# Entry of the feed-forward block: out-projection blocks in pair order, operand factors on VectorE alone, the first four up-projection blocks by direct products

## The chip, the cores and the metric

The kernel runs on one core of one Trainium2 chip. The metric is the device time of one execution in microseconds. TensorE (PE) multiplies into PSUM; VectorE (DVE), ScalarE (ACT) and GpSimd (POOL) do the elementwise work; transfers are issued by SyncE (SP).

## The reference, cut to what matters

One inference step of a two-layer decoder: 512 prompt tokens and 8 sample tokens, model width 1024, feed-forward width 4096, everything in float32. Layer 0 mixes by retention and memory attention, layer 1 by windowed attention and memory attention. Each layer then ends in the same way:

```
x = x + concat(mixer outputs) @ w_out        # the out-projection, 1024 x 1024
h = rmsnorm(x, g_mlp) @ w_up                  # 1024 -> 4096
x = x + square(relu(h)) @ w_down              # 4096 -> 1024
```

## The kernel before

Activations lie transposed: `x[kt]` is block kt (0 to 7) of 128 features by 520 tokens. All products are made of float32 values that are cut into a high part in a shorter format (a cast on ACT) and a low part (the remainder, a subtraction on DVE or POOL). Three products, high by high, high by low and low by high, replace one. Weights come by DMA as a raw block of 128 x 1024, and `chunk` cuts them in the same way (cast on line 215, remainder on line 216). There are three buffers for raw weights and three for each part.

**Out-projection.** `project` computes one output block of 128 features: 8 input blocks by 3 products for tokens 0 to 255, and the same for tokens 256 to 519, so 48 products a block. `residual` (line 434, DVE) adds each half to `x[mb]`. Layer 0 takes the blocks in the order 0 to 7. In layer 1 the first halves of blocks 0 to 6 are placed among the attention (`project_out(mb, 0)`), the second halves of these seven follow, and block 7 comes last with both halves.

**Feed-forward.** 32 up blocks are worked in four groups of eight, `up(g)`, and each group goes through `down(g)` while the next goes up. Only `up(0)` has no `down` beside it. Two up blocks are computed by `seven`: the 2 x 2 block form of a matrix product with seven sub-products in place of eight. Each sub-product is `times` (line 296): 4 input blocks by 3 products of 260 tokens, so 84 products for a pair. Sums of weight blocks are made by `total` (line 318, mostly POOL), and `parts` cuts them (cast 312, remainder 313).

The seven forms of the activations are made once per layer by `operands`. For each feature block, `y = x[kt] * gain * scale` (line 276, DVE, 520 wide), where `scale` is a factor left by the layer's first norm. From blocks j and j+4 it makes seven forms of 260 tokens: three are parts of y, four are sums or differences (`combine`, line 264). Each is cut by `cut` (cast 253 on ACT, remainder 254 on DVE or POOL by the string `ENG_L`). Of a block 0 to 3 two forms can be made alone; five forms need the second of the pair, block 4 to 7.

**Norm.** `rms` squares each `x[kt]` on ACT (line 376) and sums the squares (line 380), on the engine named by `ENG_R['f']`: POOL for blocks 1 to 6, DVE for block 7. `finish` reduces the sum over partitions on PE (line 390), runs thirteen small DVE steps (lines 393 to 361), transposes on PE (line 405) and writes the scale `r` on ACT (line 407). It is called after the first pair has been multiplied; then `u = max(u, 0) * r` (line 801, DVE), a square on ACT (line 802) and `hid.put` (cast 178, remainder 179) give the input of `down`.

**Order.** The program is handed to a planner that fixes each engine's queue before the run, by its own estimate of when things will be ready; each engine then takes its queue in order. Four PSUM banks of the kinds "mm" (three) and "ws" (two, one of which is meant here) take the up products.

Of the kernel before, what the change touches and what calls it, by code (L numbers as in the profile page):

```python
# [13 lines left out]
F32R = mybir.dt.float32r  # L14
I32 = mybir.dt.int32
AF = mybir.ActivationFunctionType
ALU = mybir.AluOpType
AX = mybir.AxisListType

P = 128  # L20
D = 1024
KT = D // P
# [8 lines left out]
SH = 12  # L31
FFG = 4
FK = 8
UK = KT // 2
EPS = 1e-6
NEG = -1e30
DK = P ** -0.5
# [2 lines left out]
ROLE_7 = ('mm', 'mm', 'ws')  # L40
BUFS_F = dict(blk=2, u=5, t=5, ws=2)
ROLE_D = ('wt', 'ot')
ORDER_F = "uddudduddudd"
ENG_UL = "vvvvvvvv"
ENG_T = "vvvp"
ENG_L = "vvpppvp"
ENG_R = dict(a='ppppvppv', m='pppppppv', f='pppppppv', b='vvvvvpvv', y='vppppppv')
ENG_B = "pvvvvvvv"
ENG_W = "pvppppvp"
BUFS_W = dict(wr=3, wh=3, wl=3)  # L50
# [66 lines left out]
def build(tc, d, o):  # L117
    nc = tc.nc
    with ExitStack() as ctx:
# [20 lines left out]
        def half(name, dt=F32, shape=None):  # L140
            return hp.tile(shape or [P, 4, TT], dt, name=name, tag="half")
# [58 lines left out]
        def gain(name, kt):  # L200
            return gains[:, GAINS.index(name), kt:kt + 1]
# [18 lines left out]
        def weights(*args, **kw):  # L220
            w, fill = chunk(*args, **kw)
            fill()
            return w

        def part(name, s, role="mm"):
            return ps(f"{name}{s}", role)[:, :HALVES[s].stop - HALVES[s].start]

        def product(t, w, act, b, s, order, nb, k):

            wh, wl = w  # L230
            for kt in order:
# [18 lines left out]
        def cut(op, j, src, eng):  # L250

            h, l = op[:, 0, j, :], op[:, 1, j, :]
            nc.scalar.copy(out=h, in_=src)  # L253
            eng.tensor_sub(out=l, in0=src, in1=f(h))  # L254

        def operands(name, g, scale):


            op, first = {}, {}
            left, right = slice(0, EVEN), slice(EVEN, TT)  # L260

            def combine(i, j, x0, x1, alu):
                t = blk(f"{name}t{i}{j}", [P, EVEN], "t")
                engine(ENG_T, (5, 7, 6, 4).index(i)).tensor_tensor(out=t, in0=x0, in1=x1, op=alu)  # L264
                put(i, j, t)
                return t

            def put(i, j, src):
                if i not in op:
                    op[i] = half(f"{name}{i}", F32R, [P, 2, UK, EVEN])  # L270
                cut(op[i], j, src, engine(ENG_L, i - 1))

            for kt in range(KT):
                j = kt % UK
                y = blk(f"{name}xg{kt}", tag="u")
                nc.vector.scalar_tensor_tensor(out=y, in0=x[kt], scalar=gain(g, kt), in1=scale, op0=ALU.mult, op1=ALU.mult)
                if kt < UK:
                    first[j] = y
                    put(1, j, y[:, left])
                    combine(5, j, y[:, right], y[:, left], ALU.subtract)  # L280
                else:
                    b11, b12, b21, b22 = first[j][:, left], first[j][:, right], y[:, left], y[:, right]
                    t = combine(7, j, b22, b12, ALU.subtract)
                    t = combine(6, j, t, b11, ALU.add)
                    put(3, j, b22)
                    combine(4, j, b21, t, ALU.subtract)
                    put(2, j, b21)
            return op
# [121 lines left out]
        def rms(name, tag="blk"):  # L410
            m = Rms(TT, TT // 5, name, tag)
            for kt in range(KT):
                m.add(kt, x[kt])
            return m
# [371 lines left out]

        def mlp(l, last):
            before, scale = now["norm"]
            op = operands(f"f{l}", f"mlp{l}", scale)
            m = rms(f"f{l}")  # L790
            r = []

            def up(g, hid):

                for n in range(0, FK, 2):
                    u = [blk(f"u{l}{g}{n}{i}", tag="u") for i in range(2)]
                    seven([d["w_up"][l, g * FK + n + i] for i in range(2)], op, u, f"u{l}{g}{n}", n // 2)
                    if not r:
                        r.append(m.finish(before)[1])
                    for i in range(2):  # L800
                        nc.vector.scalar_tensor_tensor(out=u[i], in0=u[i], scalar=0.0, in1=r[0], op0=ALU.max, op1=ALU.mult)  # L801
                        nc.scalar.square(out=u[i], in_=u[i])  # L802
                        hid.put(n + i, u[i])
                    yield

            def down(g, hid):

                for mb in range(KT):
                    w = weights(d["w_down"][l, g, mb], FK * P, f"d{l}{g}{mb}")
                    for s, ts in enumerate(HALVES):  # L810
                        t = part(f"d{l}{g}{mb}", s, ROLE_D[s])
                        product(t, w, hid, 0, s, range(FK), 1, range(FK))
                        residual(mb, ts, t)
                    yield

            def down_last(g, hid):

                ws = []
                for mb in range(KT):
                    t = half(f"dw{mb}", F32R, [P, 2, FK * P])  # L820
                    ws.append(weights(d["w_down"][l, g, mb], FK * P, f"d{l}{g}{mb}", [t[:, 0], t[:, 1]]))
                norm = iter(())
                for s, ts in enumerate(HALVES):
                    n = ts.stop - ts.start
                    m = Rms(n, n // 4, f"y{s}", "t", s == 1)
                    for mb in range(KT):
                        t = part(f"d{l}{g}{mb}", s)
                        product(t, ws[mb], hid, 0, s, range(FK), 1, range(FK))
                        residual(mb, ts, t)
                        m.add(mb, x[mb][:, ts])  # L830
                        nc.scalar.mul(out=x[mb][:, ts], in_=x[mb][:, ts], mul=gain("final", mb))
                        next(norm, None)
                    norm = final(m, s, ts)
                for _ in norm:
                    pass


            high = now["w"].tile([P, 4, 4, TT], F32R, name=f"hid{l}")

            def room(g):  # L840
                hid = Pair(f"hid{l}{g}")
                if g % 2:
                    hid.t.update({(part, i): high[:, 2 * j + i] for j, part in enumerate("hl") for i in range(2)})
                return hid

            hids = [room(g) for g in range(FFG)]
            for _ in up(0, hids[0]):
                pass
            for g in range(1, FFG):
                run(ORDER_F, u=up(g, hids[g]), d=down(g - 1, hids[g - 1]))  # L850
            if last:
                down_last(FFG - 1, hids[FFG - 1])
            else:
                for _ in down(FFG - 1, hids[FFG - 1]):
                    pass
# [9 lines left out]
        def layer_a():  # L865
# [55 lines left out]
            def memory():  # L921
# [4 lines left out]

            run(ORDER_A, h=heads(), g=(gate(h) for h in range(RH)), m=memory(), k=(step for l in range(2) for step in mem_kv(l)),
                s=mem_sample(0, qm, out), a=mem_attention(0, qm, out))
            for mb in range(KT):
                for _, ts, t in project(d["w_out_a"][mb], out, f"oa{mb}", [6, 7, 0, 1, 2, 3, 4, 5]):  # L930
                    residual(mb, ts, t)

        def layer_b():
# [44 lines left out]
            order = [6, 7, 0, 1, 2, 3, 4, 5]  # L978
            ahead = []

            def project_out(mb, s):

                if s == 0:
                    t = half(f"obw{mb}", F32R, [P, 2, KT * P]) if mb < KEEP else None
                    ahead.append(weights(*src(mb), t if t is None else [t[:, 0], t[:, 1]], nc.gpsimd if mb in POOL_W else nc.vector))
                t = part(f"ob{mb}", s)
                product(t, ahead[mb], out, 0, s, order, 1, order)
                residual(mb, HALVES[s], t)

            run(ORDER_B, k=(project_kv(i) for i in range(4)), q=(project_q(i) for i in range(6)),  # L990
                w=win_pair(0, q, kT[0], vt, out, ROLE_W), W=win_pair(1, q, kT[1], vt, out, ROLE_W),
                s=mem_sample(1, qm, out), S=win_sample(q, kT, vs, out), a=mem_attention(1, qm, out),
                o=(project_out(mb, 0) for mb in range(KEEP + 3)))
            for mb in range(KEEP + 3):
                project_out(mb, 1)
            for mb in range(KEEP + 3, KT):
                for _, ts, t in project(d["w_out_b"][mb], out, f"ob{mb}", order):
                    residual(mb, ts, t)

# [93 lines left out]
```

## Time and profile before

| | |
|---|---|
| median of three runs | 1249.92 us (1249.6 to 1253.53) |
| profiled execution, its time | 1251.94 us |
| profiled execution, its span | 1250.2 us |
| mean granted TensorE clock | 0.977 of full speed |

The profile is of one execution. Its time is 1.7 us above its span, which is what lies around the instructions. Times in rows are counted from the start of the span.

### The profile page before, as it was taken

The numbers are of one execution on the slowest core, as the hardware profiler recorded it, in microseconds if no ns is written. First come the engines' busy times: TensorE is split into PE (matmuls) and PEld (weight loads), VectorE is DVE, ScalarE is ACT, GpSimd is POOL, SyncE is SP. The second block draws the span as 40 slices with busy tenths as digits, with TensorE's granted clock in tenths as the row PEclk, the third lists the DMA queues.
The fourth block names the chain that finished last, engine by engine and source line by source line (L and its number), as shares of the span: only waits on it lengthen the run. The fifth ranks groups of instructions, "written<-read, shape, count | busy, mean of one in ns | idle before, by whom it ended". The sixth has DMA issues, their size and how long they took to land. (4 is left out here: it accounts for less than half of the span.)

```text
span 1250.2 us, 23651 instructions
## 1 busy us (share of the span) xinstructions
PE 1200.6 (96%) x9670; PEld 1140.9 (91%) x9670; DVE 853.5 (68%) x1563; ACT 537.6 (43%) x1007; POOL 310.0 (25%) x271
## 2 busy tenths in 40 slices
PE   8999999997999999999999998898999999999996
PEld 7999989997999999999999785577899999999996
DVE  7676767779876656676467548559996676666733
ACT  6232432334554444444324325554464444444532
POOL 3201100048321212121024113117632121121112
PEclk9999999999999999999999999889699999999998
DMA  8345522220222223232324353100122232322412
GB/s 306 106 154 175 201 77 85 73 85 34 102 102 102 101 86 102 85 119 85 119 85 137 103 185 128 42 1 35 51 102 102 85 118 85 105 99 92 143 37 69
DMA packets 43788, 128.25 MB, mean 103 GB/s; under 512 B 5112, under 2 KB 10368, under 8 KB 43552
## 3 DMA queue, kind: packets, MB, share of 16 engines
q1 hardware_dynamic: 41440, 119.80, 28.0%
q0 software_dynamic: 2240, 6.95, 1.5%
q8 instruction: 76, 1.25, 0.4%
q14 instruction: 32, 0.26, 0.1%
HBM read 117.65 MB, written 9.08 MB: 101 GB/s over the span
## 5 line engine op out<-in xcount | busy, mean ns | idle before, releaser
L434 DVE TENSOR_TENSOR xs<-d,xs 128x264 f32<-128x264 f32 (+1 forms) x128 | 53.9, 422 | 103.2 <-PE d L234 103.2
L802 ACT ACTIVATE u<-u 128x520 f32<-128x520 f32 x64 | 40.7, 636 | 30.3 <-DVE u L801 30.3
L234 PE MATMUL d<-hid,dw 128*128 128x256 f32 (+1 forms) x384 | 46.9, 283 | 0.0
L234 PEld LDWEIGHTS d<-hid,dw 128*128 128x128 f32 x384 | 46.3, 188 | 0.1
L635 POOL DMA_DIRECT2D out_ret_s<-s x12 | 6.8, 569 | 135.5 <-DVE s L634 102.8
L801 DVE SCALAR_TENSOR_TENSOR u<-u,f1r 128x520 f32<-128x520 f32 x32 | 30.0, 941 | 1.2 <-ACT f1r L407 0.8
L801 DVE SCALAR_TENSOR_TENSOR u<-u,f0r 128x520 f32<-128x520 f32 x32 | 29.7, 932 | 0.4
L701 POOL TENSOR_SCALAR wp<-wp,wsm 128x256 f32<-128x256 f32 (+1 forms) x32 | 15.5, 496 | 55.7 <-ACT wp L696 25.7
L234 PE MATMUL ob<-obh,obw 128*128 128x256 f32 (+1 forms) x128 | 26.7, 295 | 2.1 <-ACT obh L178 1.2
L696 ACT ACTIVATE wp<-wp,wnm 128x256 f32<-128x256 f32 (+1 forms) x48 | 22.5, 470 | 11.3 <-DVE wes L693 7.4
L234 PEld LDWEIGHTS ob<-obh,obw 128*128 128x128 f32 x128 | 21.0, 192 | 4.7 <-ACT obh L178 2.7
L179 DVE TENSOR_TENSOR hid<-u,hid 128x520 fp32r<-128x520 f32 x32 | 23.3, 729 | 0.0
L520 ACT ACTIVATE p<-ms,nm 128x256 f32<-128x256 f32 x32 | 14.8, 475 | 18.5 <-DVE nm L518 16.8
L709 PEld LDWEIGHTS wt<-c,wp 128*128 128x128 f32 x84 | 9.9, 148 | 12.6 <-POOL wp L701 6.6
L709 PE MATMUL wt<-c,wp 128*128 128x128 f32 x84 | 16.1, 302 | 5.1 <-POOL wp L701 3.5
L178 ACT CAST hid<-u 128x520 fp32r<-128x520 f32 x32 | 20.1, 628 | 0.9
L234 PE MATMUL ob<-obl,obw 128*128 128x256 f32 (+1 forms) x64 | 18.2, 299 | 0.8 <-DVE obl L179 0.7
L254 POOL TENSOR_TENSOR f<-f0t,f 128x260 fp32r<-128x260 f32 x12 | 11.8, 982 | 27.8 <-ACT f L253 27.8
L518 DVE TENSOR_REDUCE nm<-ms 128x2 f32<-128x512 f32 x16 | 10.3, 685 | 11.8 <-PE ms L499 11.8
L253 ACT CAST f<-f0t 128x260 fp32r<-128x260 f32 x16 | 6.5, 407 | 26.7 <-DVE f0t L264 26.7
L179 DVE TENSOR_TENSOR obl<-wo,obh 128x128 fp32r<-128x128 f32 x24 | 6.9, 287 | 15.1 <-ACT obh L178 15.0
L499 PE MATMUL ws<-kvb,qb 64*128 64x256 f32 (+1 forms) x96 | 15.6, 407 | 1.1 <-DVE wp L686 0.6
(2056 smaller groups left out, 5220.7 us busy)
## 6 DMA issues: line engine op xcount, KB each, us to landing
kc<-in_mem_k SPq DMA_DIRECT2D x16, 256.0 KB, 4.9
vc<-in_mem_v SPq DMA_DIRECT2D x16, 256.0 KB, 5.2
s<-in_S SPq DMA_DIRECT2D x12, 256.0 KB, 5.5
out_ret_s<-s POOLq DMA_DIRECT2D x12, 256.0 KB, 2.6
xs<-in_xT SPq DMA_DIRECT2D x8, 260.0 KB, 4.3
memx<-in_memT SPq DMA_DIRECT2D x1, 1024.0 KB, 8.8
u000r<-in_w_up SPq DMA_DIRECT2D x2, 512.0 KB, 3.2
u002r<-in_w_up SPq DMA_DIRECT2D x2, 512.0 KB, 3.2
```

Of the source, the lines that this page charges most:

```text
L178: nc.scalar.copy(out=self.hi(kt, sl, rows), in_=src)
L179: eng.tensor_sub(out=self.lo(kt, sl, rows), in0=src, in1=f(self.hi(kt, sl, rows)))
L234: nc.tensor.matmul(t, w[:, ws], a(kt, HALVES[s]), start=kt == k[0] and m == 0, stop=kt == k[-1] and m == 2)
L254: eng.tensor_sub(out=l, in0=src, in1=f(h))
L434: nc.vector.tensor_add(out=x[mb][:, ts], in0=t, in1=x[mb][:, ts])
L499: i = m()
L520: nc.scalar.activation(out=t[:, b, :], in_=s[hh][:, b, :], func=AF.Exp, bias=nm[:, b:b + 1], accum_out=sm[:, b:b + 1])
L696: nc.scalar.activation(out=pv[:, j, :], in_=pv[:, j, :], func=AF.Exp, bias=nm[:, j:j + 1], accum_out=sm[:, j:j + 1])
L701: (nc.gpsimd if j % 3 in POOL_N else nc.vector).tensor_scalar(out=pv[:, j, :], in0=pv[:, j, :], scalar1=sm[:, j:j + 1], scalar2=1.0, op0=A ...
L709: nc.tensor.transpose(t[:, i * P:i * P + P], p[:, 3 * hh + i, kk * P:kk * P + P], ident)
L801: nc.vector.scalar_tensor_tensor(out=u[i], in0=u[i], scalar=0.0, in1=r[0], op0=ALU.max, op1=ALU.mult)
L802: nc.scalar.square(out=u[i], in_=u[i])
```

## The change

The out-projection of both layers takes its blocks in the order 0, 4, 1, 5, 2, 6, 3, 7 (`BY_PAIR`), and `operands` makes its forms in that order. All remainders and combinations of `operands` and all sums of squares of this norm go to DVE; POOL has none of them. For each block `operands` also cuts the whole `y` (520 wide) into a `Pair` named `xg`, and hands `x[kt]` to the norm in the same loop. In `up(0)` the first four blocks are computed by `product` from `xg`, as an out-projection block is: 48 products each, into four PSUM banks by turns; they are evicted with the norm's `r` by one DVE operation per half. `seven` computes the last two pairs of `up(0)` and all pairs of the other groups. The buffer `high`, which held groups 1 and 3 of the hidden values, is made earlier and also holds `xg`.

```diff
+DIRECT = 2
+BY_PAIR = [kt + i * UK for kt in range(UK) for i in range(2)]
+ROLE_U = ('mm', 'mm', 'mm', 'ws')
-ENG_T = "vvvp"
-ENG_L = "vvpppvp"
-ENG_R = dict(a='ppppvppv', m='pppppppv', f='pppppppv', b='vvvvvpvv', y='vppppppv')
+ENG_R = dict(a='ppppvppv', m='pppppppv', f='vvvvvvvv', b='vvvvvpvv', y='vppppppv')
...
-        def operands(name, g, scale):
+        def operands(name, g, scale, direct, norm):
...
-                engine(ENG_T, (5, 7, 6, 4).index(i)).tensor_tensor(out=t, in0=x0, in1=x1, op=alu)
+                nc.vector.tensor_tensor(out=t, in0=x0, in1=x1, op=alu)
...
-                cut(op[i], j, src, engine(ENG_L, i - 1))
+                cut(op[i], j, src, nc.vector)
-            for kt in range(KT):
+            for n, kt in enumerate(BY_PAIR):
                 j = kt % UK
                 y = blk(f"{name}xg{kt}", tag="u")
                 nc.vector.scalar_tensor_tensor(out=y, in0=x[kt], scalar=gain(g, kt), in1=scale, op0=ALU.mult, op1=ALU.mult)
+                direct.put(kt, y)
+                norm.add(n, x[kt])
...
+            xg = room(f"xg{l}", True)
+            m = Rms(TT, TT // 5, f"f{l}", "blk")
+            op = operands(f"f{l}", f"mlp{l}", scale, xg, m)
...
-                for n in range(0, FK, 2):
+                n0 = 2 * DIRECT if g == 0 else 0
+                for n in range(n0):
+                    w = weights(d["w_up"][l, g * FK + n], D, f"u{l}{g}{n}")
+                    t = [part(f"u{l}{g}{n}", s, ROLE_U[(2 * n + s) % len(ROLE_U)]) for s in range(2)]
+                    for s in range(2):
+                        product(t[s], w, xg, 0, s, BY_PAIR, 1, BY_PAIR)
+                    if not r:
+                        r.append(m.finish(before)[1])
+                    u = blk(f"u{l}{g}{n}", tag="u")
+                    for s, ts in enumerate(HALVES):
+                        nc.vector.scalar_tensor_tensor(out=u[:, ts], in0=t[s], scalar=0.0, in1=r[0][:, ts], op0=ALU.max, op1=ALU.mult)
+                    nc.scalar.square(out=u, in_=u)
+                    hid.put(n, u)
+                    yield
+                for n in range(n0, FK, 2):
...
-            for mb in range(KT):
+            for mb in BY_PAIR:
                 for _, ts, t in project(d["w_out_a"][mb], out, f"oa{mb}", [6, 7, 0, 1, 2, 3, 4, 5]):
                     residual(mb, ts, t)
...
-            def project_out(mb, s):
+            def project_out(n, s):
+                mb = BY_PAIR[n]
...
-            for mb in range(KEEP + 3, KT):
+            for mb in BY_PAIR[KEEP + 3:]:
```

## Rows read from the trace of the kernel before

**Rows 1.** the profile page, busy time of each engine (us, share, instructions)

```profile
PE 1200.6 (96%) x9670; PEld 1140.9 (91%) x9670; DVE 853.5 (68%) x1563; ACT 537.6 (43%) x1007; POOL 310.0 (25%) x271
```

**Rows 2.** busy time by stretch; start:end, length, busy (instructions) of each engine, granted clock

```profile
294.70:328.50 33.80, 27.14 (x182) 25.57 (x181) 29.50 (x44) 16.10 (x33) 20.97 (x16) 0.85 0.14 47
328.50:351.80 23.30, 20.94 (x170) 20.32 (x169) 23.27 (x26) 14.64 (x25) 9.65 (x6) 1.00 0.27 92
351.80:361.90 10.10, 10.10 (x86) 10.10 (x86) 8.43 (x14) 6.94 (x13) 0.00 (x0) 1.00 0.33 115
868.20:906.50 38.30, 30.45 (x181) 28.81 (x181) 35.42 (x50) 18.16 (x39) 26.87 (x22) 0.73 0.14 46
906.50:929.80 23.30, 20.92 (x170) 20.29 (x169) 23.27 (x26) 14.63 (x25) 9.73 (x6) 1.00 0.26 91
```

**Rows 3.** PE's longest wait at the second entry (total us, times, longest)

```profile
PE u100b L296 <- DVE xs L434: 5.1, 1, 5.1
```

**Rows 4.** timeline, last out-projection product of layer 1, start and us

```profile
867.99 0.28 PE L234 MATMUL ob<-obh,ob7l 128*128 128x264 f32 x1
```

**Rows 5.** timeline of DVE at the second entry, residual sums

```profile
849.01 0.77 DVE L434 TENSOR_TENSOR xs<-ob,xs 128x264 f32<-128x264 f32 x2 [0.60 <-PE ob L234]
...
874.93 0.41 DVE L434 TENSOR_TENSOR xs<-ob,xs 128x256 f32<-128x256 f32 x1
```

**Rows 6.** timeline of DVE in layer 0's out-projection

```profile
272.35 0.76 DVE L276 SCALAR_TENSOR_TENSOR f0xg<-xs,gains,ar 128x520 f32<-128x520 f32 x1
273.02 1.22 DVE L216 TENSOR_TENSOR oa6l<-oa6r,oa6h 128x1024 fp32r<-128x1024 f32 x1
274.16 1.53 DVE L264 TENSOR_TENSOR f0t<-f0xg 128x260 f32<-128x260 f32 x1
275.61 0.42 DVE L254 TENSOR_TENSOR f<-f0xg,f 128x260 fp32r<-128x260 f32 x1
275.95 0.41 DVE L434 TENSOR_TENSOR xs<-oa,xs 128x256 f32<-128x256 f32 x1
```

**Rows 7.** timeline of POOL in the same stretch

```profile
273.42 1.98 POOL L380 TENSOR_TENSOR f0acc<-f0acc,f0sq 128x520 f32<-128x520 f32 x1 [2.23 <-ACT f0sq L376]
```

**Rows 8.** timeline of DVE later in that layer, two 520-wide operations

```profile
340.01 0.68 DVE L179 TENSOR_TENSOR hid00l<-u,hid00h 128x520 fp32r<-128x520 f32 x1
340.62 0.69 DVE L801 SCALAR_TENSOR_TENSOR u<-u,f0r 128x520 f32<-128x520 f32 x1
```

**Rows 9.** busy time by stretch, around the second entry

```profile
849.00:891.00 42.00, 33.58 (x218) 31.60 (x217) 41.48 (x50) 20.39 (x43) 34.52 (x29) 0.80 0.07 26
885.00:890.00 5.00, 4.98 (x24) 4.68 (x24) 4.53 (x6) 1.66 (x4) 3.92 (x4) 0.50 0.00 0
```

**Rows 10.** groups by line and shape on POOL, 849 to 891 us (busy, mean)

```profile
L254 POOL TENSOR_TENSOR f<-f1t,f 128x260 fp32r<-128x260 f32 x11 | 10.9, 995 | 1.6 <-ACT f L253 1.6
```

**Rows 11.** groups by line and shape on DVE, 849 to 891 us

```profile
L254 DVE TENSOR_TENSOR f<-f1xg,f 128x260 fp32r<-128x260 f32 x8 | 8.5, 1064 | 0.0
```

**Rows 12.** timeline of PE, seven-product pairs interleaved

```profile
903.68 0.40 PE L296 MATMUL u104a<-f,u104h 128*128 128x260 f32 x2
...
905.79 0.39 PE L296 MATMUL u104a<-f,u104l 128*128 128x260 f32 x1
```

**Rows 13.** timeline of DVE, a weight factor among the operands

```profile
286.35 0.79 DVE L276 SCALAR_TENSOR_TENSOR f0xg<-xs,gains,ar 128x520 f32<-128x520 f32 x1
287.07 1.77 DVE L313 TENSOR_TENSOR u000l<-u000r,u000h 128x1024 fp32r<-128x1024 f32 x1
```

**Rows 14.** timeline of DVE, norm chain's first and last step in layer 0

```profile
311.90 0.15 DVE L393 TENSOR_SCALAR rv<-f0ms 104x5 f32<-104x5 f32 x1
...
320.14 0.15 DVE L361 SCALAR_TENSOR_TENSOR ry<-rqt,rqu 104x5 f32<-104x5 f32 x1
```

**Rows 15.** timeline of PE, after the last gap of the second entry

```profile
891.35 0.59 PE L296 MATMUL u102a<-f,u102h 128*128 128x260 f32 x1 [0.49 <-ACT u102h L312]
...
894.98 0.33 PE L296 MATMUL u102a<-f,u102l 128*128 128x260 f32 x1
```

More of the change, by code (lines that the diff above doesn't have):

```diff
@@ L788, in mlp, with room @@
             before, scale = now["norm"]
-            op = operands(f"f{l}", f"mlp{l}", scale)
-            m = rms(f"f{l}")
+            high = now["w"].tile([P, 4, 4, TT], F32R, name=f"hid{l}")
+            def room(name, odd):
+                t = Pair(name)
+                if odd:
+                    t.t.update({(part, i): high[:, 2 * j + i] for j, part in enumerate("hl") for i in range(2)})
+                return t
+            hids = [room(f"hid{l}{g}", g % 2) for g in range(FFG)]
+            xg = room(f"xg{l}", True)
+            m = Rms(TT, TT // 5, f"f{l}", "blk")
+            op = operands(f"f{l}", f"mlp{l}", scale, xg, m)
             r = []
             def up(g, hid):
-                for n in range(0, FK, 2):
+                n0 = 2 * DIRECT if g == 0 else 0
[13 more added lines that the diff above has]
+                for n in range(n0, FK, 2):
                     u = [blk(f"u{l}{g}{n}{i}", tag="u") for i in range(2)]
                     seven([d["w_up"][l, g * FK + n + i] for i in range(2)], op, u, f"u{l}{g}{n}", n // 2)
-                    if not r:
-                        r.append(m.finish(before)[1])
                     for i in range(2):
@@ L835, in down_last @@
                     pass
[L838 to L846, printed above, removed]
             for _ in up(0, hids[0]):
@@ L979, in layer_b @@
             ahead = []
-            def project_out(mb, s):
+            def project_out(n, s):
+                mb = BY_PAIR[n]
                 if s == 0:
-                    t = half(f"obw{mb}", F32R, [P, 2, KT * P]) if mb < KEEP else None
-                    ahead.append(weights(*src(mb), t if t is None else [t[:, 0], t[:, 1]], nc.gpsimd if mb in POOL_W else nc.vector))
+                    t = half(f"obw{n}", F32R, [P, 2, KT * P]) if n < KEEP else None
+                    ahead.append(weights(*src(mb), t if t is None else [t[:, 0], t[:, 1]], nc.gpsimd if n in POOL_W else nc.vector))
                 t = part(f"ob{mb}", s)
-                product(t, ahead[mb], out, 0, s, order, 1, order)
+                product(t, ahead[n], out, 0, s, order, 1, order)
                 residual(mb, HALVES[s], t)
@@ L992, in layer_b @@
                 s=mem_sample(1, qm, out), S=win_sample(q, kT, vs, out), a=mem_attention(1, qm, out),
-                o=(project_out(mb, 0) for mb in range(KEEP + 3)))
-            for mb in range(KEEP + 3):
-                project_out(mb, 1)
-            for mb in range(KEEP + 3, KT):
+                o=(project_out(n, 0) for n in range(KEEP + 3)))
+            for n in range(KEEP + 3):
+                project_out(n, 1)
+            for mb in BY_PAIR[KEEP + 3:]:
                 for _, ts, t in project(d["w_out_b"][mb], out, f"ob{mb}", order):
```

## The prediction

> **What bounds the kernel now.** The page comes first: PE is busy 96% of the span, VectorE 68%, POOL 25% [rows 1]. A kernel like this loses time only where PE stops, so the next view is the busy time by stretch. I cut it at the two places where a feed-forward block begins, and again where each further 168 products (two pairs of up blocks, 84 each) are done. In the steady part, the third row, 84 products take 10.1 us, 0.12 us each [rows 2], so 168 should take 20.2. At layer 0's entry the first 168 take 33.8 us and the next 168 take 23.3; at layer 1's entry 38.3 and 23.3. The reader is to see three things in these rows: PE is not busy throughout, its granted clock is 0.85 and 0.73 in the first stretches, and VectorE is busy for all of the second ones. The loss against 0.12 us a product is 33.8 + 23.3 - 40.4 = 16.7 us in layer 0 and 38.3 + 23.3 - 40.4 = 21.2 us in layer 1: 38 us is all that this change can win.
>
> Then who is waited for. PE's longest wait in layer 1 is 5.1 us, put down to VectorE's residual sum [rows 3]. The timelines say why: PE issues the last out-projection product at 868.0 [rows 4], and block 7's first half, which PE finished about 3 us before that, is added to x only at 874.93 [rows 5]. VectorE's queue is in order and was about 10 us late. It was late because its operations took longer than their work. In layer 0's out-projection a 260-wide subtraction starts at 274.16 and holds VectorE for 1.45 us, while POOL runs a 520-wide sum from 273.42 to 275.40; the next 260-wide subtraction starts at 275.61, with POOL done, and the one after it follows 0.34 us later [rows 6, 7]. From 849 to 891 us VectorE is busy 41.48 of 42 us while POOL is busy 34.52 [rows 9], and its 260-wide remainders take 1064 ns on average [rows 11].
>
> **Prices.** From one start to the next, with POOL at rest: 260 wide 0.34 us (0.35 for a remainder), 520 wide 0.67 for `y` and 0.61 for a remainder, 1024 wide 1.14 [rows 6, 8]. A sum of squares, 520 wide, has no clean row; I take the 0.61 of the remainder (the upper end would be the 0.67 of `y`, 0.4 us in all). An eviction with `r` reads half a block from PSUM as the residual does: 0.42. ACT gets eight more casts of 520 a layer, at VectorE's 0.67 some 5 us, and had 21.6 of 42 us free at the busier entry [rows 9]: hidden there; without that cover it is 5 us.
>
> **What is removed and moved.** POOL gives up, in each layer, 16 remainders, 4 combinations and 6 sums of squares; they add 16 x 0.35 + 4 x 0.34 + 6 x 0.61 = 10.6 us to VectorE. Eight 520-wide remainders of `xg` add 4.9. Against that VectorE loses POOL as a neighbour. The list that it worked off from 849 to 891 is 50 instructions; at clean prices (8 of 0.67, 24 of 0.35, 9 of 0.34, four of 1.14, three of 0.61) that is 23.2 us, and it took 41.5. So sharing cost 18 us there, more than the 15.5 that come in.
>
> The Trainium skill, "Perfetto Trace Analysis", section "Optimizing Scalar/DVE Operations", speaks against the move: when VectorE is saturated, giving work to ScalarE or even GpSimd may make sense. By that half of the rule the change costs 10.6 us in layer 1, by the rows it frees 18 us. The same section warns that the two engines share a read port, so that this may not help; 1.45 against 0.34 us for one shape agrees with the warning, and I go by the rows.
>
> **What is added on PE.** Four direct blocks are 192 products instead of 168: 24 more, 2.9 us in each layer.
>
> **Layer 0, where the new wait ends.** VectorE's list for two blocks of the out-projection is now four residuals 1.36, two weight factors 2.28, two `y` 1.34, two `xg` remainders 1.22, two sums 1.22, four combinations 1.36, seven remainders 2.45: 11.2 us. PE needs 96 x 0.12 = 11.5. So it just keeps up, because pair order spreads the five-form blocks. In such a queue a weight factor finds its gap: before, the first of the up block stands right behind a `y`, among the operands [rows 13]. I expect those of u00 and u01 before PE ends the out-projection at 294.7. Block 7's `y`, cast and remainder then need 2 to 3 us, and PE has 42 products (5.0 us) of the first direct block that don't touch block 7. No wait there.
>
> The next one is the norm. The four banks hold two blocks, and a third needs an eviction, which needs `r`. Before, nothing on PE needed `r` so soon, and the thirteen steps took 8.2 us, since other work stood between them, and ended at 320.3 [rows 14], 25 us after the out-projection. Now behind block 7's residual come its list (0.67 + 0.61 + 0.61 + 1.02 + 1.75, with the residual 5.0), two weight factors 2.3 and thirteen steps of 0.2, 2.6: 9.9 us, to 304.9; transposes, ACT and the eviction some 2.3 more, 307.2. PE has 96 products and 24 of the fourth block (its second half goes to a free "ws" bank): to about 310. POOL's sums for the next pair can delay three VectorE operations by 1.1 each. I take 1.0 us of wait (bounds 0 and 4). First stage: 192 x 0.12 = 23.0, norm products 1.1, wait 1.0: 25.1 against 33.8.
>
> The two pairs after it are unchanged, but VectorE comes to them rested: four direct blocks give it 2.5 us for each 5.8 of PE. The bounds are the 23.3 of before and 20.2; between them I take 21.8. Layer 0: 46.9 against 57.1, **-10.2 us**.
>
> **Layer 1.** Here blocks 0, 4 and 1 are ready together at 849.0 [rows 5], and the others follow every 24 products, 2.9 us. Per block VectorE owes 3.3 us (0 to 3: residual, `y`, `xg`, sum, one combination, two remainders) or 5.0 (4 to 7: three combinations, five remainders). In all 4 x 3.3 + 4 x 5.0 and, for block 7, a half residual and its weight factor, less one sum: 33.9 us, so until 882.9. It never runs dry before that; the buffer for u10's weights comes free only when the sixth block is done, 72 products before 868.0, near 859, and its factor comes later in the program than all operands. I put it behind them: 884.0. Without the low part of the weights each bank can take two products: in the rows PE issues two high products for one bank, works for other banks and comes back with that bank's low one 2.1 us later; the bank's later products, high ones among them, stood behind it [rows 12]. So PE does 8 products and waits from 868.2 to 884.0: 15.8 us. The norm's chain fits into that and the next 11 us. PE then starts at half clock, 24 products in 5 us [rows 9]; before, 3.6 us of unbroken work after the last gap brought it back [rows 15], which costs 1.8. First stage: 15.8 + 184 x 0.12 + 0.6 + 1.8 = 40.3 against 38.3; pairs three and four 21.8 against 23.3. Layer 1: **+0.5 us**.
>
> **Sum.** -9.7 us on the profiled time of 1251.94 is 1242.2. That execution stood 2.0 above the median of 1249.92, so I forecast 1240.2. New SP queue order matters little: the raw weights of the next blocks wait for buffers, not for the queue. `high` moves only in memory; its first writer needs what the attention freed before the out-projection began.
>
> **Rivals.**
> A. *The factor of u10 goes ahead in layer 1.* For it: in layer 0 such a factor finds gaps. Against: the backlog. Then PE works from 868.2 on with what it has (84 products to 878.3), and the next bound is `r`: two more factors on the list 2.3, the last sum at 882, rest of the list, steps and two fillers 7.7, transposes and eviction 2: 891. PE has 120 products done, 72 are left: 899.7, with the clock 901.5. That is 33.3 instead of 40.3: 1233.2.
> B. *Layer 0 goes the way of layer 1.* The margin is 0.3 us in 11.5; if the planner puts the factors of u00 behind block 7's list, PE starts at 301.2: 6.5 + 184 x 0.12 + 0.6 + 1.8 + 21.8 = 52.8, so -4.3 in place of -10.2. With a list that is some 3 us late by the end, -1: 1246 to 1249. This is the case in which the change does little: the wait for operands has become one for weights and PE pays 2.9 us twice.
> C. *Slower: VectorE's clean prices don't hold.* At 10% more per operation layer 0's two-block list is 12.3 against 11.5 us, 2.8 late by the end, on top of B's wait, and the later pairs stay at 23.3: 9.3 + 22.1 + 0.6 + 1.8 + 23.3 = 57.1, no gain. Layer 1's list grows by 3.4: 19.2 + 22.1 + 0.6 + 1.8 + 23.3 = 67.0, +5.4: 1255.3. It decides from about 8%. For it: POOL still makes weight sums. Against: the clean rows are of this very code, and POOL's 16 remainders, 11 of them in one row [rows 10], are gone.
>
> **Chances.** Forecast 0.5, A 0.2, B 0.2, C 0.1. What one measurement of this kernel can tell from no change is 0.3%, 3.75 us: faster means below 1246.2. Forecast and A are (nearly all) faster, B mostly not: faster 0.72, within 0.3% 0.18, slower 0.10. The range reaches from A with most of what the later pairs could still give (1.6 a layer: 1230 to 1233, I take 1231) to the end of B (1250); C lies outside. The forecast's own bounds are the 4 us of `r` and 1.5 a stage in the later pairs: 1236 to 1246.
>
> **What the profile will show.** POOL idle at both entries but for weight sums, and VectorE's 260-wide remainders near 0.4 us. In layer 0 no PE gap above 1 us before the third direct block, and 25 us for the first four. In layer 1 a PE gap of over 10 us right behind the out-projection, released by the remainder of u10's weights, and VectorE's last operand near 883. Wrong would be: u10's factor before 870 (A), a gap behind layer 0's out-projection (B), or 260-wide operations still near 1 us (C).

## The result

The changed kernel takes 1239.13 us, the median of four runs (1238.24 to 1240.66), against 1250.63 (1249.6 to 1253.53) for the kernel before in four. The ratio is 0.9899, with a 95% interval of 0.9886 to 0.9912. I forecast 1240.2 with a range of 1231 to 1250. The profiled execution took 1238.24 us, with a span of 1236.4, so trace against trace the change is 13.7 us.

First the page of the changed kernel, busy time of each engine; it answers [rows 1].

```profile
PE 1196.2 (97%) x9718; PEld 1138.7 (92%) x9718; DVE 833.4 (67%) x1615; ACT 534.6 (43%) x999; POOL 229.4 (19%) x207
```

POOL has lost 80 us and 64 instructions. VectorE has gained 52 instructions and is busy 20 us *less*. Next the busy time by stretch, with the columns of [rows 2], cut at the same points of the work: out-projection to four up blocks, then to eight, in layer 0 and in layer 1.

```profile
294.90:320.90 26.00, 24.83 (x208) 24.42 (x207) 19.61 (x44) 11.47 (x20) 4.95 (x4) 1.00 0.17 62
320.90:342.20 21.30, 20.39 (x170) 20.19 (x169) 19.44 (x22) 12.76 (x21) 10.35 (x6) 1.00 0.23 75
856.50:894.70 38.20, 29.85 (x208) 28.23 (x207) 31.61 (x70) 16.96 (x33) 7.62 (x4) 0.87 0.16 56
894.70:916.10 21.40, 20.52 (x171) 20.31 (x170) 19.67 (x22) 12.88 (x21) 10.34 (x6) 1.00 0.23 75
```

Layer 0 takes 26.0 + 21.3 = 47.3 us where it took 57.1, and its clock is 1.00 throughout. Layer 1 takes 38.2 + 21.4 = 59.6 where it took 61.6: the first stage is as long as before, with the clock at 0.87. Between the two, 342.2 to 856.5, lie 514.3 us, where 516.4 lay before (351.8 to 868.2); what is behind the last stretch takes 320.3 and took 320.4. So 13.7 is 9.8 + 2.0 + 2.1, less the 0.2 by which the first stretch starts later.

**Layer 0.** The timeline of VectorE in the changed kernel: the first direct block's weight factor, among the operands as in [rows 13] and long before PE ends the out-projection at 294.9; two remainders at their clean price, 0.34 from start to start; a weight sum that waits for POOL; and the norm's first and last step, which answer to [rows 14].

```profile
284.51 1.23 DVE L217 TENSOR_TENSOR u000l<-u000r,u000h 128x1024 fp32r<-128x1024 f32 x1 [0.20 <-ACT u000h L216]
...
295.41 0.42 DVE L255 TENSOR_TENSOR f<-f0xg,f 128x260 fp32r<-128x260 f32 x1
295.75 0.42 DVE L255 TENSOR_TENSOR f<-f0t,f 128x260 fp32r<-128x260 f32 x1
...
303.09 1.75 DVE L322 TENSOR_TENSOR u004s<-u004s,u004r 128x512 f32<-128x512 f32 x1 [1.18 <-POOL u004s L322]
304.76 0.42 DVE L255 TENSOR_TENSOR f<-f0t,f 128x260 fp32r<-128x260 f32 x1
305.10 0.15 DVE L397 TENSOR_SCALAR rv<-f0ms 104x5 f32<-104x5 f32 x1
...
310.42 0.17 DVE L365 SCALAR_TENSOR_TENSOR ry<-rqt,rqu 104x5 f32<-104x5 f32 x1
```

PE's only wait of note in that stage, from its timeline, is for the eviction that needs `r`:

```profile
312.33 0.50 PE L235 MATMUL u<-hid,u002h 128*128 128x256 f32 x2 [0.98 <-DVE u L821]
```

**Layer 1.** PE's waits from 850 to 930 us (total, times, longest):

```profile
PE u L235 <- DVE hid L180: 6.1, 2, 4.1
PE u L235 <- DVE u L821: 1.0, 1, 1.0
```

The long waits of [rows 3] for a residual are gone. PE now waits for the low parts of `xg`, for blocks 3 and 7. The timeline of VectorE shows where u100's factor stands and why block 7's remainder is late:

```profile
851.89 0.75 DVE L278 SCALAR_TENSOR_TENSOR f1xg<-xs,gains,br 128x520 f32<-128x520 f32 x1
852.56 1.22 DVE L217 TENSOR_TENSOR u100l<-u100r,u100h 128x1024 fp32r<-128x1024 f32 x1
...
866.13 0.75 DVE L278 SCALAR_TENSOR_TENSOR f1xg<-xs,gains,br 128x520 f32<-128x520 f32 x1
...
869.38 0.76 DVE L255 TENSOR_TENSOR f<-f1t,f 128x260 fp32r<-128x260 f32 x2
871.30 1.74 DVE L322 TENSOR_TENSOR u104s<-u104s,u104r 128x512 f32<-128x512 f32 x1 [1.16 <-POOL u104s L322]
872.96 0.69 DVE L180 TENSOR_TENSOR hid<-f1xg,hid 128x520 fp32r<-128x520 f32 x1
873.58 1.85 DVE L255 TENSOR_TENSOR f<-f1xg,f 128x260 fp32r<-128x260 f32 x2
...
876.02 0.69 DVE L384 TENSOR_TENSOR f1acc<-f1acc,f1sq 128x520 f32<-128x520 f32 x1
...
880.26 0.15 DVE L397 TENSOR_SCALAR rv<-f1ms 104x5 f32<-104x5 f32 x1
```

Block 7's `y` starts at 866.13, but its remainder runs at 872.96: in VectorE's queue a weight sum for the *next* pair stands ahead of it, and that one waits for POOL. POOL's timeline at that place:

```profile
866.68 4.59 POOL L322 TENSOR_TENSOR u104s<-u104r 128x512 f32<-128x512 f32 x1 [40.66 <-ACT f L254]
871.24 1.25 POOL L322 TENSOR_TENSOR u104s<-u104r,u104r 128x512 f32<-128x512 f32 x1
```

Behind that wait PE runs at half clock, as the windows after it show; [rows 9] has the like of before.

```profile
875.00:880.00 5.00, 4.26 (x19) 3.73 (x19) 5.00 (x11) 2.79 (x6) 0.00 (x0) 0.50 0.09 16
880.00:885.00 5.00, 4.47 (x23) 4.09 (x21) 3.92 (x19) 0.41 (x1) 0.00 (x0) 0.53 0.53 193
```

In these ten microseconds PE issues 42 records. Short stops lie in and around them (0.25 to 0.53 us, for u103's weights, the last sum of squares and the norm's transposes). PE had one free PSUM bank left, did that bank's 24 products of u103 and the norm's own, and the remaining 72 products of the four blocks had to wait until `r` freed the other banks. ScalarE's write of `r`, and PE behind the first eviction:

```profile
885.08 0.67 ACT L411 ACTIVATE f1r<-f1mt 128x416 f32<-128x416 f32 x2 [3.21 <-PE f1mt L409]
```

```profile
886.11 0.51 PE L235 MATMUL u<-hid,u102h 128*128 128x256 f32 x2 [0.98 <-DVE u L821]
```

From there 72 products of 0.12 us take 8.6, to 894.7, where the stage ends. So `r` sets that end. The half clock ahead of it did not hold `r` back by more than some tenths: PE had added up the sums of squares for the norm by 878.66, and VectorE, whose operations stand end to end from 872.96, came to the norm's first step only at 880.26.

VectorE's 260-wide remainders in the groups from 840 to 894.7 us, for [rows 11]:

```profile
L255 DVE TENSOR_TENSOR f<-f1t,f 128x260 fp32r<-128x260 f32 x16 | 6.5, 420 | 0.0
L255 DVE TENSOR_TENSOR f<-f1xg,f 128x260 fp32r<-128x260 f32 x12 | 5.9, 511 | 0.0
```

### The profile page after: what moved, and what is told of

It reads as the page before. It is cut to its first block, busy times and chain, and to the rows that moved or that the text cites. A ratio compares the mean times of both kernels' runs of the same rounds, so it can differ in the third digit from the quotient of the medians.

```text
span 1236.4 us, 23686 instructions
## 1 busy us (share of the span) xinstructions
PE 1196.2 (97%) x9718; PEld 1138.7 (92%) x9718; DVE 833.4 (67%) x1615; ACT 534.6 (43%) x999; POOL 229.4 (19%) x207
## 3 DMA queue, kind: packets, MB, share of 16 engines
q8 instruction: 76, 1.25, 0.4%
## 5 line engine op out<-in xcount | busy, mean ns | idle before, releaser
L830 ACT ACTIVATE u<-u 128x520 f32<-128x520 f32 x56 | 35.6, 636 | 21.5 <-DVE u L829 21.5
L829 DVE SCALAR_TENSOR_TENSOR u<-u,f0r 128x520 f32<-128x520 f32 x28 | 22.7, 811 | 0.4
L829 DVE SCALAR_TENSOR_TENSOR u<-u,f1r 128x520 f32<-128x520 f32 x28 | 22.7, 811 | 0.4
L522 DVE TENSOR_REDUCE nm<-ms 128x2 f32<-128x512 f32 x16 | 10.3, 685 | 11.8 <-PE ms L503 11.8
L503 PE MATMUL ws<-kvb,qb 64*128 64x256 f32 (+1 forms) x96 | 15.6, 407 | 1.2 <-DVE wp L690 0.6
L715 ACT COPY wpT<-wt 128x384 f32<-128x384 f32 x28 | 12.8, 479 | 8.2 <-PE wt L713 7.8
L690 DVE SCALAR_TENSOR_TENSOR wp<-cb,ws 128x256 f32<-128x256 f32 (+1 forms) x48 | 15.4, 375 | 0.1
```

The lines of the kernel that those rows point to most:

```text
L503: i = m()
L690: nc.vector.scalar_tensor_tensor(out=pv[:, j, :], in0=cb["nd"][:, k0:], scalar=float(SLOPES[6 * kb + j]), in1=sv[j // 3][j % 3], op0=ALU.m ...
```

## The experiments

The table has every kernel, in order of the text. "L0" and "L1" are microseconds from the end of the out-projection's last product until the products of four up blocks, and of eight, have been issued, counted in PE's records (a record missing shifts a count by 0.12, so figures are good to about 0.5; before, they are 0.3 to 0.6 above the stretches of [rows 2]). "L1 at" is where layer 1's out-projection ends. The ratio is to runs of the kernel before on the same chip; the medians of that kernel were 1250.63, 1251.78, 1252.52 and 1251.23 there, so medians of different rows are compared to within about 2 us.

| kernel | median us | ratio, 95% | L0 four, eight | L1 at | L1 four, eight |
|---|---|---|---|---|---|
| before | 1250.63 | | 34.1, 57.5 | 868.1 | 38.8, 62.2 |
| changed | 1239.13 | 0.9899 (0.9886 to 0.9912) | 26.1, 47.4 | 856.5 | 38.2, 59.6 |
| order_alone | 1254.75 | 1.0024 (1.0015 to 1.0034) | 32.2, 57.9 | 868.1 | 38.3, 64.5 |
| vector_alone | 1246.80 | 0.9962 (0.995 to 0.9973) | 33.5, 56.4 | 863.7 | 34.9, 60.3 |
| direct_alone | 1251.41 | 0.9996 (0.9984 to 1.0007) | 31.3, 52.7 | 865.0 | 43.6, 65.0 |
| order_and_vector | 1245.66 | 0.9954 (0.9938 to 0.9971) | 30.6, 54.0 | 863.2 | 35.1, 59.1 |
| whole_pool_shares | 1250.66 | 0.9987 (0.9978 to 0.9997) | 29.8, 51.3 | 869.0 | 41.0, 62.4 |
| whole_old_order | 1239.88 | 0.9900 (0.9885 to 0.9915) | 27.2, 48.6 | 857.8 | 38.3, 59.6 |
| sums_on_vector | 1240.46 | 0.9902 (0.9884 to 0.992) | 27.2, 48.3 | 858.1 | 36.4, 57.7 |
| sums_on_pool | 1242.16 | 0.9917 (0.99 to 0.9935) | 26.5, 47.9 | 856.4 | 40.0, 61.4 |
| first_layer_only | 1241.17 | 0.9916 (0.9902 to 0.9931) | 26.2, 47.3 | 857.0 | 37.1, 62.4 |
| direct_two | 1255.44 | 1.0036 (1.0022 to 1.005) | 32.7, 57.3 | 864.8 | 43.6, 66.4 |
| late_norm | 1236.38 | 0.9879 (0.9865 to 0.9892) | 24.5, 45.8 | 854.1 | 32.1, 59.7 |
| late_norm_sums | 1232.31 | 0.9847 (0.9834 to 0.9861) | 24.5, 45.9 | 854.6 | 30.5, 56.3 |

**One part at a time.** Three kernels make one part of the change in the kernel before, and a fourth makes two.

order_alone takes the out-projection blocks, and the forms, in pair order:

```diff
-            for mb in range(KT):
+            for mb in BY_PAIR:
...
```

> Pair order alone; POOL and the seven products stay as before. Theory (VectorE's operations are slow because POOL works beside them, and that is most of the 38 us lost at the two entries): the order changes when operands come, not how long VectorE needs for them, so the mean of its 260-wide remainders at layer 1's entry stays near 1 us and the time falls by 1 to 4 us. Rival (the order does it, by spreading the blocks that owe five forms): 6 us or more off.

vector_alone moves the remainders, combinations and sums of squares to VectorE:

```diff
-ENG_T = "vvvp"
-ENG_L = "vvpppvp"
+ENG_T = "vvvv"
+ENG_L = "vvvvvvv"
-ENG_R = dict(..., f='pppppppv', ...)
+ENG_R = dict(..., f='vvvvvvvv', ...)
```

> Operands and sums of squares on VectorE alone; old order, all pairs by seven products. Theory: 260-wide remainders fall to 0.42 us, layer 1's list goes from 41.5 to about 34 us in spite of 10.6 us more work, both entries gain 5 to 9 us, 10 to 16 us off in all, as much as the whole change or more, since no extra products are paid. Rival (the direct products are what hides the operands): 4 us off or less, because PE still waits for all seven forms.

direct_alone has the four direct blocks and `xg`, with the old order and the old engines (it is the changed kernel with these two parts taken back; the lines are those that it keeps):

```diff
+                n0 = 2 * DIRECT if g == 0 else 0
+                for n in range(n0):
...
+                        product(t[s], w, xg, 0, s, BY_PAIR, 1, BY_PAIR)
```

> Direct products for the first four blocks alone; old order, operands shared with POOL as before. Theory: VectorE gets 4.9 us more work in each layer and stays slow beside POOL, PE pays 2.9 us more in each layer: between 4 us off and 4 us more. Rival (the direct products do it): 8 us off or more.

order_and_vector joins the first two:

> Pair order and VectorE alone, all pairs by seven products. Theory: as VectorE alone and 1 to 3 us better, 11 to 18 us off: then the direct products add nothing to these two. Rival (the direct products cover what is left): at least 4 us slower than the whole change, 7 us off or less.

The groups by line of VectorE at layer 1's entry, 840 to 905 us (busy, mean), from order_alone, vector_alone and direct_alone in turn:

```profile
L255 DVE TENSOR_TENSOR f<-f1xg,f 128x260 fp32r<-128x260 f32 x8 | 7.8, 990 | 0.0
```

```profile
L254 DVE TENSOR_TENSOR f<-f1t,f 128x260 fp32r<-128x260 f32 x16 | 7.6, 488 | 0.0
```

```profile
L257 DVE TENSOR_TENSOR f<-f1xg,f 128x260 fp32r<-128x260 f32 x8 | 7.7, 960 | 0.0
```

In these groups the remainders take about 1 us where POOL shares the work and under 0.5 where it doesn't, with more of them on VectorE. The parts don't add up. The order alone costs 3.0 us against the runs of the kernel before on its chip (1251.78), VectorE alone brings 5.0, direct blocks alone 0.4, which their interval doesn't part from nothing; together they bring 11.5. The theories of order_alone (1 to 4 us off) and vector_alone (10 to 16 us off) missed, that of direct_alone held, and of order_and_vector, 6.1 us off, the rival's bound held: the direct blocks cover what is left. Direct blocks alone win 4.8 in layer 0 and lose 2.8 in layer 1: `xg` gives VectorE eight more remainders beside POOL, and PE more waits. With order and VectorE in place they win 6.6 in layer 0 (54.0 to 47.4), and nothing in layer 1's own stretch (59.1 to 59.6).

**The whole change with POOL as a sharer.** whole_pool_shares is the changed kernel with the old engines for operands and squares; whole_old_order is the changed kernel with the blocks in the order 0 to 7.

```diff
-ENG_R = dict(..., f='vvvvvvvv', ...)
+ENG_R = dict(..., f='pppppppv', ...)
+ENG_T = "vvvp"
+ENG_L = "vvpppvp"
```

> The whole change, but operands and sums of squares shared with POOL as before. Theory (the parts need one another: direct products pay only when VectorE works at its clean price): 4 to 10 us slower than the whole change, 1243 to 1250, with 260-wide remainders near 1 us again. Rival (once the direct products are there, VectorE's price no longer counts, since the seven forms have 23 us more): within 2 us of the whole change.

```diff
-BY_PAIR = [kt + i * UK for kt in range(UK) for i in range(2)]
+BY_PAIR = list(range(KT))
```

> The whole change, but with the blocks in the order 0 to 7. Theory (pair order spreads the blocks that owe five forms; without it blocks 4 to 7 bring 5.0 us of list each, one after the other): layer 0 gets a wait of 1 to 4 us behind the out-projection, layer 1 two to four us more than the whole change has: 3 to 7 us slower than the whole change. Rival (order by itself did nothing, so it does nothing here): within 1.5 us of it.

Giving POOL its share back costs 11.5 us by the medians, 11.0 by the two ratios, and leaves 0.9987 of the kernel before: the theory had it so, though at 4 to 10 us. Its remainders on VectorE at layer 1's entry:

```profile
L257 DVE TENSOR_TENSOR f<-f1xg,f 128x260 fp32r<-128x260 f32 x8 | 6.6, 830 | 0.0
```

The old order makes no difference that can be told in the whole (0.9900 and 0.9899), though its one trace has layer 0 at 48.6 for 47.4; the theory of 3 to 7 us fell. The pair order, to which the prediction gave part of layer 0's margin, isn't needed for the gain.

**The weight sums at layer 1's wait.** Two kernels move the sums of the first seven-product pair of `up(0)`, in both layers, to one engine.

```diff
             def total(i, x0, x1, alu):
-                engine(ENG_W, i, turn).tensor_tensor(
+                (nc.vector if alone else engine(ENG_W, i, turn)).tensor_tensor(
```

> The whole change with the four weight sums of the first seven-product pair after the direct blocks on VectorE, POOL having none of them. Theory (in layer 1 the remainder of xg's last block stands in VectorE's queue behind a weight sum that waits for POOL's, and POOL's took 4.59 us because VectorE had the port): the waits of 4.1 us in layer 1 and 1.0 us in layer 0 fall to under 2 and under 0.5, 2 to 5 us better than the whole change, 1234 to 1237. Rival (VectorE has no room, whatever it does: the four sums are 2.4 us more on its list): within 1 us of the whole change or slower.

sums_on_pool has `nc.gpsimd` in that place:

> The whole change with all four of these sums on POOL. Theory (the wait is the order in the queue, and sharing costs some more): VectorE no longer stands behind POOL, but its operations beside POOL stay slow: 0.5 to 3 us better than the whole change, and 1 to 3 us slower than with the sums on VectorE. Rival (only the queue counted, sharing costs nothing here): as good as with the sums on VectorE.

On VectorE the sums win 1.9 us in layer 1 and lose 0.9 in layer 0, where they lengthen a list that was in time; the two medians can't be told apart (1240.46 and 1239.13). The theory had counted on 2 to 5 us in all and fell. On POOL they cost 1.8 in layer 1, where the theory had counted on a gain, and the ratio is 0.9917, which the intervals part neither from 0.9899 nor from the 0.9902 of the sums on VectorE.

**Direct blocks in layer 0 only, and fewer of them.** first_layer_only leaves layer 1 to the seven products; direct_two makes two blocks direct in place of four.

```diff
-                n0 = 2 * DIRECT if g == 0 else 0
+                n0 = 2 * DIRECT if g == 0 and l == 0 else 0
```

> The whole change, but direct products only in layer 0; layer 1 forms its first four up blocks from the seven products, with the pair order and VectorE alone, and makes no remainders of `xg`. Theory (in layer 1 the direct blocks bring nothing: with order and VectorE alone that entry took 59.05 us up to the end of the second pair of stages, in the whole change 59.58, because VectorE's list is the bound in both): layer 0 keeps its 47.4, layer 1 comes to 58 to 60.5, total within 2 us of the whole change, 1237.5 to 1241. Rival (the direct blocks do hide part of layer 1's list; the near equality came from the later start of layer 0's rest): layer 1 goes to 63 or more, total 1243 or more.

```diff
-DIRECT = 2
+DIRECT = 1
```

> Two direct blocks a layer in place of four. Theory (the second pair of direct blocks pays 1.44 us of extra products a layer and buys VectorE the time for the operands and the weight sums of the next pair): layer 0 loses more than it saves, since the sums of u002 and u003 and their four factors, 1.2 to 1.7 us each, come to VectorE while it still works on the last operands and the norm: PE waits 3 to 6 us there, layer 0 at 49 to 52; layer 1 about the same, 58 to 62; total 1240 to 1245. Rival (the extra products are what counts, the sums are in time): 2 x 1.44 us less, 1236 to 1237.

first_layer_only keeps layer 0 and takes 2.0 us more in all, 0.2 outside the theory's range and below the rival's; layer 1 takes 62.4, 2.8 more. The intervals of the two kernels overlap, so the direct blocks of layer 1 bring some 2 us by the medians, and perhaps nothing.

In direct_two both sides were wrong. It wins nothing of the 2.9 us and takes 16.3 more than the changed kernel, more than the whole change gives. PE's waits in layer 0 (295 to 330 us) and in layer 1 (850 to 900):

```profile
PE f0mt L409 <- DVE ry L365: 5.5, 1, 5.5
...
PE f1mt L409 <- DVE ry L365: 9.8, 1, 9.8
```

PE stands at the norm's transposes, and the banks hold products that can't leave without `r`. The steps, from VectorE's timeline of that kernel in layer 0, with three that take over a microsecond instead of 0.17:

```profile
306.44 0.16 DVE L397 TENSOR_SCALAR rv<-f0ms 104x5 f32<-104x5 f32 x1
...
308.45 1.27 DVE L364 TENSOR_TENSOR rqt<-rqt,rqu 104x5 f32<-104x5 f32 x1
...
311.85 1.23 DVE L365 SCALAR_TENSOR_TENSOR rqu<-rqt,rqu 104x5 f32<-104x5 f32 x1
313.11 1.18 DVE L363 TENSOR_TENSOR rqt<-rqu,rv 104x5 f32<-104x5 f32 x1
...
314.53 0.17 DVE L365 SCALAR_TENSOR_TENSOR ry<-rqt,rqu 104x5 f32<-104x5 f32 x1
```

Two things come together in that wait. PE had 108 products to do before it (96 direct ones and 12 of the seven products' first pair) where the changed kernel has 120, and ran out 13.9 us after the out-projection, 2.4 earlier than there. And the last step ended 3.8 us later than there, 19.4 us after the out-projection for 15.6: the three slow steps make 3.2 of it. They run beside POOL's weight sums for the pair of u04. In layer 1 the sums for u02's pair run beside VectorE's operands too. How the 16.3 us divide between the lost products and the sums and factors that moved wasn't tried by itself.

**Without the wait for `r`.** late_norm lets ScalarE copy the direct blocks out of PSUM, and VectorE applies `r` afterwards from SBUF, 520 wide.

```diff
-                        nc.vector.scalar_tensor_tensor(out=u[:, ts], in0=t[s], scalar=0.0, in1=r[0][:, ts], op0=ALU.max, op1=ALU.mult)
+                        nc.scalar.copy(out=u[:, ts], in_=t[s])
+                    nc.vector.scalar_tensor_tensor(out=u, in0=u, scalar=0.0, in1=r[0], op0=ALU.max, op1=ALU.mult)
```

> The whole change; the direct blocks leave PSUM by a copy on ScalarE that doesn't need the norm's factor `r`, and VectorE applies `r` in one 520-wide operation from SBUF. Theory (PE's wait for `r` is about 1 us in each layer and nothing else hangs on it): layer 0's first four blocks 25.0 to 25.6 in place of 26.05, layer 1's 37 to 38; total 0.5 to 2.5 us below the whole change, 1236.7 to 1238.7. Rival (`r` also holds back the work on VectorE behind it, or the late norm keeps PE's clock low after the wait): 3 us or more per entry where it matters, total below 1236.

late_norm_sums adds the sums on VectorE, in layer 1 alone (`l == 1 and n == n0 and g == 0`):

> The late norm, and in layer 1 only the four weight sums of the first seven-product pair on VectorE instead of partly on POOL. Theory (PE's waits for the last `xg` remainders in layer 1 come from VectorE standing in front of a sum that POOL is still making; 1.9 us were saved there by this edit before, while layer 0 lost 0.9): layer 1's first two stages 56 to 58 in place of 59.58, layer 0 as with the late norm alone; total 1.5 to 4 us below the whole change, 1235 to 1237.5. Rival (VectorE's list has no room: what the sums free, they take): the same as the late norm alone within 0.7 us.

late_norm is 2.8 us below the changed kernel (the two intervals overlap a little), just past the theory of a small wait, but not in its way. Busy time by stretch in layer 1, four blocks and then four more, of late_norm:

```profile
854.10:886.20 32.10, 26.00 (x203) 25.50 (x202) 29.38 (x60) 14.86 (x32) 9.98 (x5) 0.95 0.21 68
886.20:913.80 27.60, 23.87 (x175) 23.45 (x174) 21.45 (x28) 17.05 (x30) 6.37 (x4) 0.88 0.15 52
```

The first stage is 6.1 us shorter, the rival's size: the same 6.1 us of waits for `xg` stand in it, but behind them PE has products for all four blocks and goes on without a stop to the end of the stage, with the clock at 0.95 in place of 0.87. That its waits and the gain are both 6.1 is chance. The second stage is 6.2 longer than in the changed kernel, and its clock is 0.88: PE now gets there early and waits, 3.2 us in one piece, for the weight factors of u106:

```profile
PE u106a L300 <- ACT u106h L316: 3.2, 1, 3.2
```

So the gain of layer 1 was turned into a new wait, and what remains is layer 0's 1.6 us and 0.8 on the way to layer 1. With the sums on VectorE the second stage gives back less. The same two stretches of late_norm_sums, and its sum and remainder at VectorE:

```profile
854.60:885.10 30.50, 26.08 (x203) 25.57 (x202) 28.29 (x58) 14.73 (x32) 2.73 (x2) 0.94 0.23 70
885.10:910.90 25.80, 22.75 (x175) 22.34 (x174) 21.66 (x32) 16.89 (x30) 5.93 (x4) 0.93 0.18 62
```

```profile
866.25 0.69 DVE L322 TENSOR_TENSOR u104s<-u104r 128x512 f32<-128x512 f32 x1
...
869.42 0.69 DVE L180 TENSOR_TENSOR hid<-f1xg,hid 128x520 fp32r<-128x520 f32 x1
```

At 1232.31 us this is the fastest kernel of the study, below both sides' expectations: 4.1 below late_norm, where the sums without the late norm (in both layers) had won nothing. Ratio to the kernel before 0.9847, with an interval that doesn't touch that of the changed kernel.

## Why the prediction was right, point by point

**The price of sharing.** It held. The 260-wide remainders went from 1064 ns [rows 11] to 420 and 511 in their two groups at that entry, and taking the change of engines back loses 11.0 to 11.5 us, nearly all of the gain. (The clean list of 23.2 us counts 48 of the 50 instructions, so the 18 us are a little high.) Alone the change of engines brought 5.0 us, so the clean prices are needed for the gain, not enough for it.

**Layer 0, -10.2.** Measured -9.8. The two halves are 26.0 for 25.1 and 21.3 for 21.8. The factors of u00 and u01 were placed as forecast, before 294.9, and no wait stands at block 7. The 1.0 us for `r` came out (0.98) by luck, for its working did not: I had the eviction at 307.2 and PE busy until about 310, which leaves no wait, and took 1.0 between bounds of 0 and 4. The eviction came at 311.85, because two weight remainders of 1.2 us stand among the norm's steps, and a sum of 1.75, itself 1.18 late by POOL, just ahead of them; PE's products lasted to 311.4. Direct_two shows how much hangs on that balance: with 12 products fewer before it and the chain 3.8 us later PE waits 5.5 us for the norm, and the layer takes 57.3.

**Layer 1, +0.5.** Measured -2.0, and this is the step that failed: "its factor comes later in the program than all operands. I put it behind them: 884.0." It stands at 852.56, four microseconds *before* the out-projection ends, as rival A had it. So the 15.8 us of wait at its start weren't there, and PE worked on until 865.9. But A's 33.3 us didn't come either; it took 38.2. A had the placing right, and `r` as the next bound, but set it too early: PE going on 22.8 us after the out-projection, where it goes on 29.6 after it (886.11). From there both count the same 72 products; A adds 1.8 for a low clock, which was back at 1.00 by then (885 to 890). A's last sum of squares stood 13.8 us after PE's end, the measured one 19.5 (876.02), and 3.9 us of this difference lie beside POOL: 2.8 in the weight sum ahead of block 7's remainder (870.1 to 872.96), 1.1 in the two remainders at 873.58. PE's 6.1 us of waits for the low parts of `xg`, blocks 3 and 7, and the ten microseconds at half clock stand ahead of `r` and don't set the end.

Other kernels agree. Counted from the end of layer 1's out-projection, PE goes on behind `r` after 29.5 us in whole_old_order, 27.7 in sums_on_vector, 32.3 in whole_pool_shares and 34.9 in direct_alone, and in each the four blocks are done 8.9 us later; in sums_on_pool it is 29.9 and 10.3, with the clock at 0.53 from 885 to 890. Late_norm takes the wait for `r` away, and the stage takes 32.1. So a second step of the forecast failed as well, "The norm's chain fits into that and the next 11 us", and that 40.3 and 38.2 lie so near is luck: a wait of 15.8 us that wasn't there stands against a bound that was taken as covered.

**Between the layers, 0.** Measured -2.1; I had no term for it. It goes with the engines: counted from the end of layer 0's eight blocks to the end of layer 1's out-projection, it takes 512.4 to 515.1 us in the ten kernels with VectorE alone, the old block order among them, and 515.4 to 520.7 in the four in which POOL shares (before: 515.9). In the last 10 us before layer 1's entry the traces show where half of it lies. PE's wait there in the kernel before, for the low part of block 7's weights:

```profile
PE ob L234 <- DVE ob7l L216: 0.9, 1, 0.9
```

No kernel with VectorE alone has it, and the other three in which POOL shares wait 0.6 to 0.9 us there: layer 1's first operands are in VectorE's queue already, and with POOL that weight remainder comes late. The other half lies further back, in waits that differ from kernel to kernel, and stays open.

**The sum.** -9.7 forecast, 13.7 by the traces, 11.5 by the medians. I had taken the profiled execution of before as 2.0 above its median; later runs had it at 1250.63, and the profiled one of after is 0.9 below its own. That is why a sum which is 4 us off trace against trace lies within 1.1 us of the median, and it is luck. The two errors, layer 1's and that between the layers, have the same sign.

**The rivals.** B and C fell: layer 0 kept up, and VectorE's clean prices held. A is half true: the placing and the kind of bound, not its time.

## What to carry to other kernels

Before work is spread over two engines, look whether the same shape has two durations in the trace: here taking 10.6 us of work back from POOL freed VectorE. Work that looks like a surcharge (24 products more a layer) can pay for itself elsewhere: halving it lost more than the whole change had won, for PE ran out of products earlier and the norm's chain, with other operations moved beside it, ended later. So ask what PE does while the norm is made, and what else moves, before pricing its products. A wait that PE shows need not be the one that sets a stage's end: in layer 1 the waits for operands and the half clock stood ahead of `r`, and `r` alone counted. And where one wait goes, read the next stage in the same way: late_norm won 6.1 us in one stage and gave 6.2 back in the following one, until the sums there had been moved as well.

## What the runs showed of the hardware

VectorE and POOL did not slow one another by a share; their operations on SBUF took turns. In the changed kernel POOL's sum starts at 866.68 and lasts 4.59 us, while VectorE runs its operations end to end at clean prices until 870.1; from there the sum needs 1.1 us, near to what the next one takes (1.25). The other way round, a VectorE operation that starts at 274.16 in the kernel before ends at 275.69, 0.29 behind POOL's, which had begun first [rows 6, 7]. The three slow steps of the norm in direct_two show it best; POOL's timeline at their place:

```profile
308.42 1.28 POOL L322 TENSOR_TENSOR u004s<-u004r 128x512 f32<-128x512 f32 x1 [14.49 <-DVE rqt L363]
311.33 1.72 POOL L322 TENSOR_TENSOR u004s<-u004r,u004r 128x512 f32<-128x512 f32 x1 [1.64 <-DVE rqt L364]
313.01 1.25 POOL L322 TENSOR_TENSOR u004s<-u004r,u004s 128x512 f32<-128x512 f32 x1
```

These end at 309.70, 313.05 and 314.26; the three steps of 104 by 5 elements end at 309.72, 313.08 and 314.29. A step that takes 0.17 us lasts as long as what is left of POOL's operation. The Trainium skill, "SBUF — State Buffer", section "Who interferes with whom", says that a VectorE instruction with two SBUF inputs contends with a POOL instruction that reads SBUF, that the port pair which they share is an exclusive lock, and that the order of issue decides who blocks. The traces agree in all five places that the two take turns. In the first of them the order of the recorded starts does not decide: POOL's sum is on record from 866.68, and eight VectorE operations that start after it, from 866.80 on, end before it. What I had not expected is this loss of POOL's: behind VectorE operations that stand end to end, its sum of 1.25 us took 4.59.
